# A row-mean kernel: the first load behind the entry barrier again, and the last row cut into columns of 704, 192 and 128

## The chip, the cores and the metric

The kernel runs on one core of a Trainium2 chip. Times are device microseconds of one execution. Three runs of the kernel before gave 163.88, 164.01 and 164.14 us; the median is 164.01. A profiled execution is read beside them.

## The reference

```python
def setup_inputs():
    batch, seq, dim = 32, 512, 1024
    return {"x": np.random.randn(batch, seq, dim).astype(np.float32)}

def reference(x):
    relu_x = np.maximum(x, 0)
    return np.mean(relu_x, axis=-1).astype(np.float32)
```

For each of 16384 rows of 1024 fp32 numbers the negative ones are set to zero and the mean is taken. The input is 67.1 MB, the output 64 KB.

## The kernel before

**Tiling.** The rows are laid out with 128 rows of `j` to each of 128 partitions: `J` is 128, and partition p holds rows 128 p to 128 p + 127. A tile `xt` takes 16 such rows per partition (`NB`, line 63), 128 x 16 x 1024 numbers, 8 MB. There are eight tiles and three buffers for them (line 72).

**Loads.** All loads are issued by SyncE. Seven tiles come in one DMA each (line 92). The eighth is cut finer and finer so that little work is left when the last byte lands: pieces of 8, 4, 2 and 1 rows (`row_pieces`, line 100), and the last row of each partition in three column pieces of 512, 256 and 256 (`col_pieces`, line 104). A load into a buffer waits until VectorE and ScalarE are done with the tile that was there.

**Compute.** Each row of a partition is one instruction that takes the maximum with zero in place and sums the row: odd rows on VectorE (`dve_row`, line 20), even rows on ScalarE (`act_row`, line 15). Each such instruction shows as two in the profile, the operation and a read of its accumulator. The sums go to a column of `sums`. GpSimd multiplies the sums by 1/1024 in two goes (`finish`, line 85): the first 112 columns once seven tiles are done, and 14 more in the last tile. The last two rows go their own way through the small tile `part`:

- The row before the last (`prev`) is halved between ScalarE and VectorE (lines 116 and 117); GpSimd adds the two parts and scales (line 118).
- The last row's first 512 columns are halved between ScalarE and VectorE (lines 121 and 122). GpSimd scales ScalarE's part (line 123). The next 256 are halved again (lines 126 and 127); VectorE's instruction takes its sum of the 256 before as a starting value (`init`), so it must wait for it. ScalarE adds its own part, scaled, to GpSimd's (line 128). The last 256 columns are VectorE's (line 131), started with the sum so far. VectorE's line 132 scales its sum and adds ScalarE's.

Line 135 stores the whole result, `res`, from SyncE.

**What sets the order.** Each engine takes its instructions in the order in which they were written, and semaphores set by the framework make an instruction wait for what it reads. At the start, line 155 (the program's creation) gives a few instructions ahead of the kernel's own: four GpSimd memsets of constants, and an entry barrier at which all five engines drain, report and wait for release. By hand, `issue_ahead_of_entry_barrier` (lines 26 to 42) takes SyncE's first load out of the kernel's body once all is compiled, and puts it in front of SyncE's drain at that barrier. The load waits for nothing, and its consumers wait for its semaphore.

Of the kernel before, what the change touches and what calls it, by code (L numbers as in the profile page):

```python
# [1 line left out]

# [4 lines left out]

F32 = mybir.dt.float32
ALU = mybir.AluOpType
ACT = mybir.ActivationFunctionType  # L10


def act_row(nc, src, acc):

    nc.scalar.activation(out=src, in_=src, func=ACT.Relu, accum_out=acc)  # L15


def dve_row(nc, src, acc, init=None):

    nc.vector.tensor_scalar(  # L20
        out=src, in0=src, scalar1=0.0, scalar2=init,
        op0=ALU.max, op1=ALU.add, accum_out=acc,
    )


def issue_ahead_of_entry_barrier(nc):


    entry, body = nc.cur_f.blocks[0].instructions, None
    for block in nc.cur_f.blocks[1:]:  # L30
        for k, ins in enumerate(block.instructions):
            if ins.opcode == "DMACopy":
                body, load = block.instructions, k
                break
        if body is not None:
            break
    first = body[load]
    assert first.engine == mybir.EngineType.SP and not first.sync_info.on_wait
    assert all(i.opcode == "DMACopy" or i.engine != first.engine for i in body[:load])
    del body[load]  # L40
    at = next(k for k, i in enumerate(entry) if i.engine == first.engine and i.opcode == "Drain")
    entry.insert(at, first)


@with_exitstack
def kernel(
    ctx: ExitStack,
    tc: tile.TileContext,
    x: bass.AP,
    out: bass.AP,  # L50
):
    nc = tc.nc
    P = nc.NUM_PARTITIONS
    xf = x.flatten_outer_dims()
    R, D = xf.shape
    assert R % P == 0
    J = R // P
    inv = 1.0 / D
    xr = xf.rearrange("(p j) d -> p j d", p=P, j=J)
    outr = out.flatten().rearrange("(p j) -> p j", p=P, j=J)  # L60
    xlast = xr[:, J - 1, :]

    NB = 16
    full = J // NB - 1

    row_pieces = [8, 4, 2, 1]
    assert sum(row_pieces) == NB - 1
    col_pieces = [512, 256, 256]
    assert sum(col_pieces) == D

    pools = ctx.enter_context(ExitStack())
    in_pool = pools.enter_context(tc.tile_pool(name="in", bufs=3))
    res_pool = pools.enter_context(tc.tile_pool(name="res", bufs=1))
    sums = res_pool.tile([P, J], F32)
    res = res_pool.tile([P, J], F32)
    part = res_pool.tile([P, 10], F32)

    def rows(xt, lo, n, j0):

        for k in range(lo, lo + n):  # L80
            j = j0 + k
            (dve_row if j % 2 else act_row)(nc, xt[:, k, :], sums[:, j:j + 1])

    def finish(lo, hi):
        nc.gpsimd.tensor_scalar(  # L85
            out=res[:, lo:hi], in0=sums[:, lo:hi], scalar1=inv, scalar2=0.0, op0=ALU.mult, op1=ALU.add,
        )

    for t in range(full):
        j0 = t * NB  # L90
        xt = in_pool.tile([P, NB, D], F32, name="xt")
        nc.sync.dma_start(out=xt, in_=xr[:, j0:j0 + NB, :])  # L92
        rows(xt, 0, NB, j0)

    j0 = full * NB
    xt = in_pool.tile([P, NB, D], F32, name="xt")
    prev, last = xt[:, NB - 2, :], xt[:, NB - 1, :]
    lo = 0
    for n in row_pieces:
        nc.sync.dma_start(out=xt[:, lo:lo + n, :], in_=xr[:, j0 + lo:j0 + lo + n, :])  # L100
        lo += n
    c = 0
    for w in col_pieces:
        nc.sync.dma_start(out=last[:, c:c + w], in_=xlast[:, c:c + w])
        c += w

    finish(0, j0)
    lo = 0
    for n in row_pieces[:-1]:
        rows(xt, lo, n, j0)  # L110
        lo += n
    finish(j0, j0 + lo)

    act_row(nc, prev[:, :512], part[:, 0:1])
    dve_row(nc, prev[:, 512:], part[:, 1:2])
    nc.gpsimd.tensor_scalar(  # L118
        out=res[:, J - 2:J - 1], in0=part[:, 0:1], scalar1=part[:, 1:2], scalar2=inv, op0=ALU.add, op1=ALU.mult,
    )  # L120
    act_row(nc, last[:, :256], part[:, 2:3])
    dve_row(nc, last[:, 256:512], part[:, 3:4])
    nc.gpsimd.tensor_scalar(  # L123
        out=part[:, 4:5], in0=part[:, 2:3], scalar1=inv, scalar2=0.0, op0=ALU.mult, op1=ALU.add,
    )
    act_row(nc, last[:, 512:640], part[:, 5:6])
    dve_row(nc, last[:, 640:768], part[:, 6:7], init=part[:, 3:4])
    nc.scalar.activation(  # L128
        out=part[:, 7:8], in_=part[:, 5:6], func=ACT.Identity, scale=inv, bias=part[:, 4:5],
    )  # L130
    dve_row(nc, last[:, 768:], part[:, 8:9], init=part[:, 6:7])
    nc.vector.scalar_tensor_tensor(  # L132
        out=res[:, J - 1:J], in0=part[:, 8:9], scalar=inv, in1=part[:, 7:8], op0=ALU.mult, op1=ALU.add,
    )
    nc.sync.dma_start(out=outr, in_=res)

    pools.close()
    tc.close()
    tc.compile()
    issue_ahead_of_entry_barrier(nc)  # L140


# [1 line left out]
_INS = ['x']  # L144
_OUTS = [((32, 512), 'float32')]


# [23 lines left out]
```

## Time and profile before

| | us |
|---|---|
| median of three runs | 164.01 |
| profiled execution | 163.88 |
| its span, first to last instruction | 162.1 |
| outside the span | 1.8 |
| VectorE busy | 74.7 |
| ScalarE busy | 69.6 |
| GpSimd busy | 1.2 |
| first tile landed | 22.34 |
| last column piece landed | 158.62 |
| last VectorE operation ends | 159.58 |

The times in the lower rows count from the span's start, which is SyncE's first load. Per row of 1024 columns VectorE takes 1.22 us and ScalarE 1.04 us. The DMA queue of the loads carries 67.18 MB, a mean of 415 GB/s over the span.

### The profile page before, as it was taken

The numbers are of one execution on the slowest core, as the hardware profiler recorded it, in microseconds if no ns is written. First come the engines' busy times: TensorE is split into PE (matmuls) and PEld (weight loads), VectorE is DVE, ScalarE is ACT, GpSimd is POOL, SyncE is SP. The second block draws the span as 40 slices with busy tenths as digits, with TensorE's granted clock in tenths as the row PEclk, the third lists the DMA queues.
The fourth block names the chain that finished last, engine by engine and source line by source line (L and its number), as shares of the span: only waits on it lengthen the run. The fifth ranks groups of instructions, "written<-read, shape, count | busy, mean of one in ns | idle before, by whom it ended". The sixth has DMA issues, their size and how long they took to land.

```text
span 162.1 us, 358 instructions
## 1 busy us (share of the span) xinstructions
DVE 74.7 (46%) x135; ACT 69.6 (43%) x134; POOL 1.2 (1%) x8
## 2 busy tenths in 40 slices
DVE  0000049700795009930199102990049800698993
ACT  3000049500793009910199002980049600696882
POOL 0000000000000000000000000000000000000001
DMA  8996996997997998998998999899898897998980
GB/s 275 501 485 291 518 501 291 501 501 323 469 518 340 437 518 356 420 518 356 420 520 374 404 501 404 388 501 404 388 518 388 388 518 332 437 445 384 420 311 17
DMA packets 2162, 67.19 MB, mean 415 GB/s; under 512 B 240, under 2 KB 624, under 8 KB 880
## 3 DMA queue, kind: packets, MB, share of 16 engines
q1 hardware_dynamic: 2160, 67.18, 96.6%
q14 instruction: 2, 0.02, 0.0%
HBM read 67.11 MB, written 0.07 MB: 414 GB/s over the span
## 4 chain that ended last, share of the span: by engine, by line
DMA 84%; DVE 13%; SPq 1%; issue 0%; DVEq 0%
DMA xt<-in_x_dram 84%; DVE xt L20 13%; SPq L100 1%; DVE res L132 0%; DVEq L20 0%; DVEq L132 0%; SPq L92 0%
## 5 line engine op out<-in xcount | busy, mean ns | idle before, releaser
L20 DVE TENSOR_SCALAR_CACHE_REDUCE xt<-xt 128x1024 f32<-128x1024 f32 (+1 forms) x65 | 73.7, 1195 | 84.7 <-DMA xt<-in_x_dram 84.3
L15 ACT ACTIVATE xt<-xt 128x1024 f32<-128x1024 f32 (+1 forms) x66 | 67.0, 1015 | 88.7 <-DMA xt<-in_x_dram 88.6
L15 ACT ACTIVATION_READ_ACCUMULATOR xt<-xt 128x1 f32 x66 | 12.3, 186 | 0.0
L20 DVE DVE_READ_ACCUMULATOR xt<-xt 128x1 f32 x65 | 5.4, 83 | 0.0
L85 POOL TENSOR_SCALAR res<-sums 128x112 f32<-128x112 f32 (+1 forms) x2 | 0.5, 252 | 156.7 <-DVE xt L20 156.7
L15 ACT ACT_TABLE_LOAD x1 | 1.3, 1283 | 0.8 <-PEq L155 0.8
L20 DVE TENSOR_SCALAR_CACHE_REDUCE xt<-xt,part 128x128 f32<-128x128 f32 (+1 forms) x2 | 0.8, 412 | 0.1
L128 ACT ACTIVATE part<-part 128x1 f32<-128x1 f32 x1 | 0.3, 294 | 0.1
L118 POOL TENSOR_SCALAR res<-part 128x1 f32<-128x1 f32 x1 | 0.3, 264 | 0.5 <-ACT xt L15 0.5
L132 DVE SCALAR_TENSOR_TENSOR res<-part 128x1 f32<-128x1 f32 x1 | 0.2, 159 | 0.1
L123 POOL TENSOR_SCALAR part<-part 128x1 f32<-128x1 f32 x1 | 0.2, 191 | 0.1
L20 DVE DVE_READ_ACCUMULATOR xt<-xt,part 128x1 f32 x2 | 0.2, 83 | 0.0
L155 POOL MEMSET const-bfloat16-1.0<- 128x1 bf16 x1 | 0.1, 101 | 0.0
L155 POOL MEMSET const-uint8-127<- 128x1 uint8 x1 | 0.1, 101 | 0.0
L155 POOL MEMSET const-float32-0.0<- 128x1 f32 x1 | 0.1, 98 | 0.2 <-issue 0.2
L155 POOL MEMSET const-float32-1.0<- 128x1 f32 x1 | 0.1, 98 | 0.0
## 6 DMA issues: line engine op xcount, KB each, us to landing
xt<-in_x_dram SPq DMA_DIRECT2D x1, 4096.0 KB, 39.0
xt<-in_x_dram SPq DMA_DIRECT2D x1, 2048.0 KB, 43.5
xt<-in_x_dram SPq DMA_DIRECT2D x1, 1024.0 KB, 45.5
xt<-in_x_dram SPq DMA_DIRECT2D x1, 512.0 KB, 46.4
xt<-in_x_dram SPq DMA_DIRECT2D x1, 256.0 KB, 46.5
xt<-in_x_dram SPq DMA_DIRECT2D x2, 128.0 KB, 42.7
xt<-in_x_dram SPq DMA_DIRECT2D x7, 49.1
out_dram<-res SPq DMA_DIRECT2D x1, 64.0 KB, 1.5
```

Of the source, the lines that this page charges most:

```text
L15: nc.scalar.activation(out=src, in_=src, func=ACT.Relu, accum_out=acc)
L20: nc.vector.tensor_scalar(out=src, in0=src, scalar1=0.0, scalar2=init, op0=ALU.max, op1=ALU.add, accum_out=acc,)
L85: nc.gpsimd.tensor_scalar(out=res[:, lo:hi], in0=sums[:, lo:hi], scalar1=inv, scalar2=0.0, op0=ALU.mult, op1=ALU.add,)
L100: nc.sync.dma_start(out=xt[:, lo:lo + n, :], in_=xr[:, j0 + lo:j0 + lo + n, :])
L118: nc.gpsimd.tensor_scalar(out=res[:, J - 2:J - 1], in0=part[:, 0:1], scalar1=part[:, 1:2], scalar2=inv, op0=ALU.add, op1=ALU.mult,)
L123: nc.gpsimd.tensor_scalar(out=part[:, 4:5], in0=part[:, 2:3], scalar1=inv, scalar2=0.0, op0=ALU.mult, op1=ALU.add,)
L128: nc.scalar.activation(out=part[:, 7:8], in_=part[:, 5:6], func=ACT.Identity, scale=inv, bias=part[:, 4:5],)
L132: nc.vector.scalar_tensor_tensor(out=res[:, J - 1:J], in0=part[:, 8:9], scalar=inv, in1=part[:, 7:8], op0=ALU.mult, op1=ALU.add,)
L155: nc = _bacc.Bacc("TRN2", target_bir_lowering=False, num_devices=1)
```

## The change

The changed kernel no longer moves the first load: `issue_ahead_of_entry_barrier` is gone, and so are the lines that closed the pools and compiled the program by hand ahead of it (the framework does both when the function returns). The last row comes in column pieces of 704, 192 and 128. ScalarE takes 416 columns of the first piece and VectorE 288; the other two pieces are VectorE's alone. No instruction starts with an earlier sum: each writes its own part. GpSimd adds the first three parts (new line 104) while VectorE works on the last piece, and VectorE adds the fourth part and scales (new line 108).

```diff
-def issue_ahead_of_entry_barrier(nc):
...
-    first = body[load]
...
-    del body[load]
-    at = next(k for k, i in enumerate(entry) if i.engine == first.engine and i.opcode == "Drain")
-    entry.insert(at, first)
...
-    col_pieces = [512, 256, 256]
+    col_pieces = [704, 192, 128]
...
-    act_row(nc, last[:, :256], part[:, 2:3])
-    dve_row(nc, last[:, 256:512], part[:, 3:4])
+    act_row(nc, last[:, :416], part[:, 2:3])
+    dve_row(nc, last[:, 416:704], part[:, 3:4])
+    dve_row(nc, last[:, 704:896], part[:, 4:5])
     nc.gpsimd.tensor_scalar(
-        out=part[:, 4:5], in0=part[:, 2:3], scalar1=inv, scalar2=0.0, op0=ALU.mult, op1=ALU.add,
+        out=part[:, 5:6], in0=part[:, 4:5], scalar1=part[:, 3:4], scalar2=part[:, 2:3], op0=ALU.add, op1=ALU.add,
     )
-    act_row(nc, last[:, 512:640], part[:, 5:6])
-    dve_row(nc, last[:, 640:768], part[:, 6:7], init=part[:, 3:4])
-    nc.scalar.activation(
-        out=part[:, 7:8], in_=part[:, 5:6], func=ACT.Identity, scale=inv, bias=part[:, 4:5],
-    )
-    dve_row(nc, last[:, 768:], part[:, 8:9], init=part[:, 6:7])
-    nc.vector.scalar_tensor_tensor(
-        out=res[:, J - 1:J], in0=part[:, 8:9], scalar=inv, in1=part[:, 7:8], op0=ALU.mult, op1=ALU.add,
+    dve_row(nc, last[:, 896:], part[:, 6:7])
+    nc.vector.tensor_scalar(
+        out=res[:, J - 1:J], in0=part[:, 6:7], scalar1=part[:, 5:6], scalar2=inv, op0=ALU.add, op1=ALU.mult,
     )
     nc.sync.dma_start(out=outr, in_=res)
-
-    pools.close()
-    tc.close()
-    tc.compile()
-    issue_ahead_of_entry_barrier(nc)
```

More of the change, by code (lines that the diff above doesn't have):

```diff
@@ L23, in dve_row @@
     )
-def issue_ahead_of_entry_barrier(nc):
[L29 to L36, printed above, removed]
-    first = body[load]
-    assert first.engine == mybir.EngineType.SP and not first.sync_info.on_wait
-    assert all(i.opcode == "DMACopy" or i.engine != first.engine for i in body[:load])
-    del body[load]
-    at = next(k for k, i in enumerate(entry) if i.engine == first.engine and i.opcode == "Drain")
-    entry.insert(at, first)
 @with_exitstack
@@ L67 @@
     assert sum(row_pieces) == NB - 1
-    col_pieces = [512, 256, 256]
+    col_pieces = [704, 192, 128]
     assert sum(col_pieces) == D
-    pools = ctx.enter_context(ExitStack())
-    in_pool = pools.enter_context(tc.tile_pool(name="in", bufs=3))
-    res_pool = pools.enter_context(tc.tile_pool(name="res", bufs=1))
+    in_pool = ctx.enter_context(tc.tile_pool(name="in", bufs=3))
+    res_pool = ctx.enter_context(tc.tile_pool(name="res", bufs=1))
     sums = res_pool.tile([P, J], F32)
```

## The prediction

> **What bounds the kernel now.** I read the slices of the page and the DMA share by stretches first, then the chain that ended last, then the two ends of the span instruction by instruction. The DMA share (columns: stretch, its length, busy VectorE, ScalarE and GpSimd, clock, DMA share, GB/s):
>
> ```profile
> 0.90:1.00 0.10, 0.00 (x0) 0.10 (x1) 0.00 (x0) 1.00 0.00 0
> 1.00:1.05 0.05, 0.00 (x0) 0.05 (x1) 0.00 (x0) 1.00 3.98 1311
> ...
> 2.00:138.00 136.00, 55.23 (x96) 50.60 (x97) 0.00 (x0) 1.00 0.99 428
> ```
>
> From 2 to 138 us the DMA engines are 0.99 busy and VectorE is busy for 55 us of 136. So the input stream runs without a hole: whatever delays its first byte delays every byte, and the compute engines have the slack to follow. The first byte moves at 1.01 us, one microsecond after the first issue at 0.00. The start, on SyncE and on ScalarE:
>
> ```profile
> 0.00 0.38 SPq L92 DMA_DIRECT2D xt<-in_x_dram  x1
> 0.78 0.33 SPq L92 DMA_DIRECT2D xt<-in_x_dram  x1
> 0.78 1.28 ACT L15 ACT_TABLE_LOAD   x1 [0.78 <-PEq L155]
> ```
>
> The first load goes out at 0.00, and the second only at 0.78, when the entry barrier (line 155) has let all engines go. The end of the span:
>
> ```profile
> 156.05 1.22 DVE L20 TENSOR_SCALAR_CACHE_REDUCE xt<-xt 128x1024 f32<-128x1024 f32 x1
> 157.19 0.08 DVE L20 DVE_READ_ACCUMULATOR xt<-xt 128x1 f32 x1
> 157.34 0.69 DVE L20 TENSOR_SCALAR_CACHE_REDUCE xt<-xt 128x512 f32<-128x512 f32 x1
> 157.95 0.08 DVE L20 DVE_READ_ACCUMULATOR xt<-xt 128x1 f32 x1
> 157.97 0.42 DVE L20 TENSOR_SCALAR_CACHE_REDUCE xt<-xt 128x256 f32<-128x256 f32 x1
> 158.32 0.08 DVE L20 DVE_READ_ACCUMULATOR xt<-xt 128x1 f32 x1
> 158.44 0.35 DVE L20 TENSOR_SCALAR_CACHE_REDUCE xt<-xt,part 128x128 f32<-128x128 f32 x1
> 158.71 0.08 DVE L20 DVE_READ_ACCUMULATOR xt<-xt,part 128x1 f32 x1
> 158.83 0.48 DVE L20 TENSOR_SCALAR_CACHE_REDUCE xt<-xt,part 128x256 f32<-128x256 f32 x1
> 159.23 0.08 DVE L20 DVE_READ_ACCUMULATOR xt<-xt,part 128x1 f32 x1
> 159.43 0.16 DVE L132 SCALAR_TENSOR_TENSOR res<-part 128x1 f32<-128x1 f32 x1
> ```
>
> The row before the last lands at 157.31 (in the chain: a DMA of 46.35 us from 110.96). The three column pieces are issued at 111.44, 111.93 and 119.59 and land 46.5, 46.4 and 39.0 us later: at 157.95, 158.31 and 158.62. The final operation ends at 159.58, so 0.96 us lie between the last byte and the last sum; then comes the store (issue at 159.65, landing 1.5 us later), and the span ends at 162.1.
>
> **Part 1: the first load goes back behind the barrier.** In the changed kernel's order of instructions SyncE passes the barrier's wait and then issues all seven big loads. The first issue takes the place that the second one has now, 0.78 us. It may be a little earlier: SyncE's drain, which the 0.38 us issue holds up, is the last arrival at the barrier (it ends at 0.56), and GpSimd's own drain after its four memsets ends at 0.49; without the early issue the barrier opens up to 0.07 us sooner. So the issue moves by 0.71 to 0.78 us; I take 0.71. From issue to first byte the trace has two rows: 1.01 us for this load, 0.84 us for the store (issue 159.65, first byte 160.49). If the load's longer time is a cold start that the wait at the barrier hides, 0.17 us come back. Lower bound of the shift 0.54, upper 0.78, taken **+0.71**, by the first row, which is the same load. Nothing covers it: the stream has no hole to absorb it. Loads 2 and 3 follow 0.38 and 0.8 us behind as now, and stand in the queue behind 19 us of transfer; load 4 goes out at 31.65, when a buffer is free, 29 us before load 3 has landed (61.0), and the later ones likewise. ScalarE's table load ends at 2.06, 20 us before the first data. No SyncE instruction is passed but the barrier's drain and wait.
>
> The Trainium skill ("DMA: Bandwidth & Descriptors", section Latency and other measured facts) gives about 600 ns to the first byte of a load issued from SyncE; the trace has 1010. If the page's figure held behind the barrier, the shift would be 0.71 + 0.60 - 1.01 = 0.30 us, an estimate from that page; I go by the row.
>
> **Part 2: column pieces 704, 192, 128.** The same 512 KB in the same three DMAs, so the last byte keeps its place, 158.62. The row's pieces took 1.31 us (157.31 to 158.62) for 1024 columns; in proportion 704 land after 0.90, at 158.21, and 192 at 158.46. Both engines, free at 157.97 and 158.02, now wait for the first piece until about 158.23; in before they begin at 157.97.
>
> **Part 3: the compute on the last row.** VectorE rows without a `part` input: 1024 columns 1.22 us, 512 0.69, 256 0.42, so 1.04 ns a column and 0.15 fixed; that makes 0.45 for 288, 0.35 for 192 and 0.285 for 128. In rows that wait for nothing the next one starts 0.07 us before the end of the one before (1.14 apart at 1.22 long). So 288 runs 158.23 to 158.68, 192 to 158.96, 128 to 159.17, its sum out at 159.18. What is removed is the wait of each piece for the sum of the one before: 0.04 us instead of -0.07 between pieces, and 0.06 us for reading `part` (0.48 against 0.42 for 256). ScalarE's 416 columns (rows 0.63 for 512, 0.42 for 256) take 0.55 and the accumulator read reaches 0.09 beyond: done at 158.87, ahead of VectorE's 192. ScalarE's two last operations (lines 126 and 128) go, off the path.
>
> The new wait: GpSimd's add of three parts (new line 104) stands behind VectorE's 192 sum at 158.97. Two GpSimd rows that wait for VectorE start 0.14 to 0.16 after it (157.43 after 157.28; 158.20 after ScalarE at 158.06): start 159.12. Its length is in no row: 0.19 with two constants (line 123), 0.26 with one pointer (line 118), so between 0.19 and 0.34 with two pointers (0.07 more for the second); I take 0.30: 159.42. VectorE's last operation waits for it; semaphore to start is 0.06 (SyncE's store behind line 132) to 0.11 (ScalarE's line 128 behind line 123): 159.48 to 159.53. VectorE's own 128 sum would allow 159.18 + 0.11 = 159.29, so **GpSimd ends last, not VectorE**. The last operation is 0.16 by line 132, up to 0.22 if its pointer costs what it cost the 256 piece. End 159.64 to 159.75, against 159.58. Bounds for the tail: below, all low values, 159.05 + 0.19 + 0.06 + 0.16 = 159.46, or -0.12; above, +0.20. Taken **+0.06**. Behind it only SyncE's store is queued, which moves with it.
>
> The Trainium skill ("Perfetto Trace Analysis", section GPSIMD Engine Instruction) says to treat GpSimd spans as unreliable and go by start to start. ScalarE's line 128 starts 0.30 us after GpSimd's line 123, at most 0.11 us after its shown end, so the trace has no hidden end there; by starts alone the add would cost 0.30 + 0.07 and the tail some +0.06 to +0.1.
>
> **Sum.** 0.71 + 0.06 = +0.77 us on the profiled execution's 163.88: 164.65 (its span would grow less, since the span begins with the first instruction, which is now no longer the load). The median of the three runs stands 0.13 above that execution, 164.01, so the forecast is 164.01 + 0.77, about **164.8**.
>
> **Rivals.**
> 1. *An instruction fetch sets the end (not slower).* Tiles land every 19.32 to 19.35 us, but 80.36 to 100.22 is 19.86: 0.51 more, the stretch in which the page's two packets of queue q14 fall. The 0.51 us stays to the end. If in the changed program the fetch falls where it doesn't hit the DMA engine that is last, 0.51 comes back: 0.71 + 0.06 - 0.51 = +0.26, 164.27, no measurable change. It decides from 0.44 us given back. Against it: VectorE and ScalarE run the same 126 row operations in the same order until the last row, so they fetch at the same place. Chance 0.07. The Trainium skill ("Runtime: NRT & Kernel Launch", section Instruction fetch mechanics) calls the fetch mostly hidden; by it this rival is worth nothing, and the row of 0.51 us disagrees.
> 2. *Half the start is hidden.* The first packets take longer than later ones: the first tile lands at 22.34, 21.3 us after its first byte, against 19.35 for later tiles. If part of this ramp is a clock of its own and not part of the load, up to 0.4 us of it could run beside the barrier: 164.4. For: 2 us of ramp is much. Against: nothing moves bytes before the issue. Chance 0.07.
> 3. *The tail is dearer*: GpSimd's two-pointer add takes 0.5 us or more, or its start lags: +0.3 and more, 165.05 to 165.3. Chance 0.07.
> 4. *Faster*: the early issue brings nothing now (the queue not ready before 1.0 us, whatever the issue) and independent sums save 0.12: at most 163.9 to 163.6. Against it: the store's row shows at least 0.84 us from issue to byte, so a load issued at 0.71 cannot move before 1.55. Chance 0.03.
>
> **How the numbers follow.** The forecast has 0.76. Its own bounds are 164.01 + 0.54 - 0.12 = 164.43 and 164.01 + 0.78 + 0.20 = 164.99, with 0.13 us of spread between runs on each side at worst; the range 164.35 to 165.1 holds it and parts of rivals 2 and 3, about 0.83 in all. A measurement tells 0.2% from no change, 0.33 us, so slower means above 164.34. Rival 1 and a small part of 2 fall within (0.09), rival 4 gives 0.03 faster, the rest 0.88 slower.
>
> **What would show it.** Right: the SyncE row of the first load behind the barrier, with the bytes 1.0 us behind it; the final VectorE operation released by GpSimd's line 104, about 1.0 us after the last column piece. Wrong: bytes less than 0.8 us after the issue (part 1), tile landings without the 19.86 step (rival 1), a last operation that starts straight behind VectorE's 128 piece (part 3).

## The result and the profile after

The changed kernel takes 164.69 us (median of four runs, 164.59 to 165.03) against 163.97 for the one before in the same measurement; the ratio is 1.0046, interval 1.0028 to 1.0064. That is slower by 0.72 us; the forecast was 0.79 (164.8 against 164.01). Its profiled execution took 164.59 us with a span of 162.8; the one before took 163.88 with 162.1. Both spans begin at the same moment of the entry (VectorE's drain lies 0.13 us behind it in both), so times within the spans may be compared.

The start, DMA share by stretches as before, then the first issue on SyncE and the table load on ScalarE:

```profile
1.60:1.70 0.10, 0.00 (x0) 0.10 (x1) 0.00 (x0) 1.00 0.00 0
1.70:1.75 0.05, 0.00 (x0) 0.05 (x1) 0.00 (x0) 1.00 8.13 2621
...
2.00:138.00 136.00, 55.23 (x96) 50.55 (x97) 0.00 (x0) 1.00 0.99 428
```

```profile
0.73 0.38 SPq L72 DMA_DIRECT2D xt<-in_x_dram  x1
0.73 1.28 ACT L15 ACT_TABLE_LOAD   x1 [0.73 <-PEq L126]
```

The issue has moved from 0.00 to 0.73 us, the first byte from 1.01 to 1.74. The barrier opens 0.05 us sooner than before (the table load starts at 0.73 instead of 0.78), where up to 0.07 was forecast, since SyncE no longer comes to it late. The stream is as full as it was: 0.99, 428 GB/s.

The last row, in order of time (start, length, engine and line):

```profile
157.92 0.69 DVE L20 TENSOR_SCALAR_CACHE_REDUCE xt<-xt 128x512 f32<-128x512 f32 x1
158.53 0.08 DVE L20 DVE_READ_ACCUMULATOR xt<-xt 128x1 f32 x1
...
158.82 0.45 DVE L20 TENSOR_SCALAR_CACHE_REDUCE xt<-xt 128x288 f32<-128x288 f32 x1 [0.21 <-DMA xt<-in_x_dram]
...
159.20 0.35 DVE L20 TENSOR_SCALAR_CACHE_REDUCE xt<-xt 128x192 f32<-128x192 f32 x1
159.28 0.19 ACT L15 ACTIVATION_READ_ACCUMULATOR xt<-xt 128x1 f32 x1
159.47 0.08 DVE L20 DVE_READ_ACCUMULATOR xt<-xt 128x1 f32 x1
159.47 0.28 DVE L20 TENSOR_SCALAR_CACHE_REDUCE xt<-xt 128x128 f32<-128x128 f32 x1
159.68 0.08 DVE L20 DVE_READ_ACCUMULATOR xt<-xt 128x1 f32 x1
159.73 0.36 POOL L104 TENSOR_SCALAR part<-part 128x1 f32<-128x1 f32 x1 [0.68 <-DVE xt L20]
160.13 0.21 DVE L108 TENSOR_SCALAR res<-part 128x1 f32<-128x1 f32 x1 [0.37 <-POOL part L104]
```

VectorE now waits 0.21 us for the first column piece. Its pieces follow each other without a gap, and its last sum is out at 159.76, but it then stands idle for 0.37 us until GpSimd's add of three parts is done at 160.10. The column pieces land at 158.80, 159.01 and 159.20, so from the last landing to the end of the last operation (160.35) it is 1.15 us, against 0.97 before.

Put together, after against before in these two executions: first byte +0.73; first tile landed +0.83 (23.17 against 22.34), so 0.10 more from the first byte to the first landing; the stretch between the fourth and the fifth tile 19.61 instead of 19.86, so -0.25; last column piece +0.58; the work behind it +0.18; the store and the exit -0.05. The sum is +0.71, the whole difference of 164.59 and 163.88.

### The profile page after: what moved, and what is told of

Read it like the earlier page. It is cut to its first block, busy times and chain, and to the rows that moved or that the text cites. A ratio compares the mean times of both kernels' runs of the same rounds, so it can differ in the third digit from the quotient of the medians.

```text
span 162.8 us, 353 instructions
## 1 busy us (share of the span) xinstructions
DVE 74.5 (46%) x135; ACT 69.2 (43%) x131; POOL 1.3 (1%) x8
## 4 chain that ended last, share of the span: by engine, by line
DMA 84%; DVE 12%; SPq 1%; issue 0%; POOLq 0%; DVEq 0%
DMA xt<-in_x_dram 84%; DVE xt L20 12%; SPq L80 1%; POOLq L137 0%; SPq L72 0%; DVE res L108 0%; DVEq L20 0%; POOLq L104 0%
## 5 line engine op out<-in xcount | busy, mean ns | idle before, releaser
L20 DVE TENSOR_SCALAR_CACHE_REDUCE xt<-xt 128x1024 f32<-128x1024 f32 (+2 forms) x67 | 74.2, 1169 | 85.5 <-DMA xt<-in_x_dram 85.1
```

Source lines behind the costliest of these rows:

```text
L20: nc.vector.tensor_scalar(out=src, in0=src, scalar1=0.0, scalar2=init, op0=ALU.max, op1=ALU.add, accum_out=acc,)
```

## The experiments

Eleven runs. "Tail" is the time from the last landing to the end of the last operation in the run's profile.

| run | load | tail in the profile, us | time, us | ratio to before, interval |
|---|---|---|---|---|
| before | ahead of the barrier | 0.97 | 163.81 to 163.97 | |
| after | behind | 1.15 | 164.69 | 1.0046, 1.0028 to 1.0064 |
| e1_load_behind | behind | 0.98 | 164.33 | 1.0038, 1.0026 to 1.0050 |
| e2_tail_alone | ahead | 1.14 | 163.98 | 1.0012, 1.0004 to 1.0021 |
| e3_two_parts | ahead | 1.06 | 163.88 | 1.0012, 1.0002 to 1.0022 |
| e7_one_piece | ahead | 0.83 | 163.74 | 0.9992, 0.9983 to 1.0001 |
| e5_scalar_ends | ahead | 0.78 | 163.73 | 0.9990, 0.9980 to 0.9999 |
| e12_scalar_again | ahead | 0.78 | 163.60 | 0.9986, 0.9977 to 0.9995 |
| e6_few_rows (no compute on two tiles) | ahead | 0.98 | 164.01 | 1.0010, 1.0001 to 1.0020 |
| e9_fewest_rows (no compute on four tiles) | ahead | 0.99 | 163.98 | 1.0003, 0.9994 to 1.0012 |
| e8_load_later | behind a memset | 0.98 | 166.91 | 1.0179, 1.0165 to 1.0194 |
| e10_first_row | 1 row ahead | 0.81 | 163.57 | 0.9985, 0.9969 to 1.0000 |
| e11_first_four | 4 rows ahead | 0.81 | 163.27 | 0.9965, 0.9954 to 0.9977 |

**Start alone and tail alone.** The first run undoes only the early issue in the kernel before:

```diff
     tc.compile()
-    issue_ahead_of_entry_barrier(nc)
```

> The kernel before, with only the moving of the first load taken away. Theory (start and tail add up): the first issue at about 0.73 us, the first byte 1.0 us behind it, every landing later by 0.7 to 0.85, the work behind the last column piece unchanged at 0.96 us; time +0.55 to +0.85 us over before. Rival (the start is partly hidden and the new tail is most of the loss): +0.1 to +0.4 us.

The second keeps the early issue and takes the new tail. Against the changed kernel it puts the early issue back:

```diff
+def issue_ahead_of_entry_barrier(nc):
...
+    pools.close()
+    tc.close()
+    tc.compile()
+    issue_ahead_of_entry_barrier(nc)
```

> The changed kernel, with the first load ahead of the barrier as before: the new tail alone. Theory: 1.15 us from the last landing to the end of the last operation as in the changed kernel, 0.18 more than before, so +0.1 to +0.25 us if the last landing stays. Rival (the tail costs nothing, all is the start): within 0.05 us of before. Second rival (the tail is most of the loss): +0.4 us or more.

Behind the barrier alone costs a ratio of 1.0038, 0.62 us; the new tail alone 1.0012, 0.20 us. Their sum, 0.82, agrees with the 0.75 of both together (1.0046) within the intervals. The start is about three quarters of that sum, and the rivals of both runs fall: the start is neither mostly hidden nor the smaller part, and the tail is not free. The issue stands at 0.74 and the first byte at 1.75 in the first run; in the second the tail is that of the changed kernel instruction by instruction. One thing in the first run missed: every landing was to come 0.7 to 0.85 us later, but in the profiled executions the first tile lands 0.56 later (22.90) and the last piece 0.42 (159.04). From first byte to first landing it took 21.15 us there, in the kernel before 21.33; that differs from run to run, as the next run shows too.

**A larger dose of the start.** The load waits, behind the barrier, for a VectorE memset of cells that it then fills (so do the next two loads):

```diff
+        if t < 3:
+            nc.vector.memset(xt[:, 0:2, :], 0.0)
         nc.sync.dma_start(out=xt, in_=xr[:, j0:j0 + NB, :])
...
-    issue_ahead_of_entry_barrier(nc)
```

> The kernel before without the early issue, and the first three loads wait besides for a VectorE memset of 2048 columns each in the tiles they fill (nothing left out). Theory (the input stream has no hole, so the start goes into the time one for one): the first byte 1.0 us behind the issue, and the last landing later than with the load merely behind the barrier by as much as the issue is later (1.1 to 2.2 us by the memset's unknown length), within 0.35 us for the ramp. Rival (a ramp with a clock of its own): the first tile's landing moves by less than half of what the issue moves.

The first rows on VectorE and SyncE:

```profile
1.24 1.76 DVE L93 MEMSET xt<- 128x2048 f32 x1 [1.24 <-PEq L156]
3.03 4.61 SPq L94 DMA_DIRECT2D xt<-in_x_dram  x3
```

The issue is at 3.03, 2.29 us later than merely behind the barrier; the first byte is at 4.05. By the ratios the kernel takes 2.93 us more than before (2.70 to 3.18), and 2.31 more than with the load merely behind the barrier. So the start goes into the time one for one, as near as these intervals tell. From first byte to first landing it takes 21.6 us here, 21.2 (first run) and 21.4 (changed kernel) behind the barrier, and 21.1 to 21.4 in the kernels with the uncut load ahead: it is no shorter when the load waits, so no part of it runs beside the barrier. In the profiled executions the last landing is later by 2.72 us than in the first run, 0.43 more than the issue, where at most 0.35 was expected; 0.40 of it is the longer time to the first landing.

**Who ends the tail.** The three-part add is taken apart: GpSimd adds the two parts of the first piece only, and VectorE reads the 192 sum as one more cell of the last piece. For that the 192 columns are now the row's last ones, and are loaded ahead of the 128. Against the kernel with the new tail alone:

```diff
...
-    for w in col_pieces:
...
+    for lo, hi in ((0, 704), (832, 1024), (704, 832)):
...
-    dve_row(nc, last[:, 704:896], part[:, 4:5])
     nc.gpsimd.tensor_scalar(
-        out=part[:, 5:6], in0=part[:, 4:5], scalar1=part[:, 3:4], scalar2=part[:, 2:3], op0=ALU.add, op1=ALU.add,
+        out=part[:, 5:6], in0=part[:, 2:3], scalar1=part[:, 3:4], scalar2=inv, op0=ALU.add, op1=ALU.mult,
     )
-    dve_row(nc, last[:, 896:], part[:, 6:7])
+    dve_row(nc, last[:, 832:], last[:, 703:704])
+    dve_row(nc, last[:, 703:832], part[:, 6:7])
...
```

> The new tail with the load ahead of the barrier, but GpSimd adds only the two parts of the first piece (one pointer, no need of the 192 columns), and VectorE carries the 192 sum into the last piece by a column in front of it. Theory (GpSimd's add of three parts, waiting for the 192 sum, ends last): the last operation is released by VectorE's own last piece, 0.75 to 0.95 us from the last landing to its end, 0.2 to 0.4 less than with three parts. Rival (VectorE's own chain sets the end, the wait for GpSimd is only named last): no less than 1.1 us.

```profile
158.36 0.35 DVE L20 TENSOR_SCALAR_CACHE_REDUCE xt<-xt 128x192 f32<-128x192 f32 x1
158.60 0.26 POOL L119 TENSOR_SCALAR part<-part 128x1 f32<-128x1 f32 x1 [0.51 <-ACT xt L15]
158.64 0.08 DVE L20 DVE_READ_ACCUMULATOR xt<-xt 128x1 f32 x1
158.75 0.29 DVE L20 TENSOR_SCALAR_CACHE_REDUCE xt<-xt 128x129 f32<-128x129 f32 x1
158.97 0.08 DVE L20 DVE_READ_ACCUMULATOR xt<-xt 128x1 f32 x1
159.16 0.16 DVE L124 SCALAR_TENSOR_TENSOR res<-part 128x1 f32<-128x1 f32 x1
```

GpSimd is done at 158.86 and no longer in the way, yet the tail is 1.06, between the 0.75 to 0.95 of my theory and the 1.1 of its rival. VectorE's own waits take the place: the 192 columns start at 158.36 instead of right behind the 288 at 158.24, since they write a cell that the 288 wrote, and the 129 start 0.04 us behind the end of the 192 instead of 0.07 ahead of it. Counted from the start of the 288 the last piece begins 0.89 us later, in the changed tail 0.65. That eats what GpSimd's add cost there: VectorE's own sum was out at 159.76, and 0.11 us later (the step to line 132 in the kernel before) its last operation could have started, 0.26 us sooner than it did; this is an estimate from those rows. So GpSimd's add does end the changed tail, but this edit gains only 0.08 us in the tail, and none in the time.

**A tail without those waits.** If waits from sum to sum are the cost and columns are not, fewer instructions are better. First, 192 and 128 as one piece; GpSimd adds the two parts of the first piece, as in the run before:

```diff
-    col_pieces = [704, 192, 128]
+    col_pieces = [704, 320]
...
+    dve_row(nc, last[:, 704:], part[:, 6:7])
...
```

> The load ahead of the barrier; the last row in pieces of 704 and 320; the 320 are one VectorE instruction that waits for no earlier sum, GpSimd adds the two parts of the first piece and VectorE adds the rest. Theory (the tail is paid in waits from sum to sum, some 0.1 us each, and not in columns): 0.80 to 0.90 us from the last landing to the end of the last operation, against 1.14 in the changed tail, 0.97 in the one before and 1.06 with two parts and a third piece; released by GpSimd or VectorE within 0.1 us of one another; time 0.05 to 0.2 us under before. Rival (columns after the last landing set the tail): 320 columns in one pass are 0.2 us more than 128, so 1.1 us or more.

```profile
158.47 0.49 DVE L20 TENSOR_SCALAR_CACHE_REDUCE xt<-xt 128x320 f32<-128x320 f32 x1
158.82 0.27 POOL L123 TENSOR_SCALAR part<-part 128x1 f32<-128x1 f32 x1 [0.49 <-ACT xt L15]
158.88 0.08 DVE L20 DVE_READ_ACCUMULATOR xt<-xt 128x1 f32 x1
159.12 0.16 DVE L127 SCALAR_TENSOR_TENSOR res<-part 128x1 f32<-128x1 f32 x1 [0.15 <-POOL part L123]
```

Then ScalarE as the last engine: the two sums of the first piece go into the two cells ahead of the second one, and one scaled ScalarE instruction sums cells and columns straight into the result.

```diff
+    head = 448
...
+    act_row(nc, flat[:, mid:c0 + D], flat[:, c0 - 2:c0 - 1])
+    dve_row(nc, flat[:, c0 + head:mid], flat[:, c0 - 1:c0])
+    end = flat[:, c0 - 2:c0 + head]
+    nc.scalar.activation(out=end, in_=end, func=ACT.Relu, scale=inv, accum_out=res[:, J - 1:J])
```

> The load ahead of the barrier; the last row in two pieces of 576 and 448, in that order; ScalarE and VectorE sum 288 columns each of the first and put their sums into the two cells in front of the second piece, and one ScalarE instruction sums those cells and the 448 columns, scaled, into the result. No GpSimd or VectorE work behind the last landing. Theory (waits from engine to engine are the tail): 0.70 to 0.80 us from the last landing to the end, the shortest of all tails; time 0.1 to 0.3 us under before. Rival (the ScalarE pass of 450 columns eats what the waits give back): 0.97 us or more, time as before.

```profile
158.44 0.58 ACT L124 ACTIVATE xt<-xt 128x450 f32<-128x450 f32 x1
158.92 0.19 ACT L124 ACTIVATION_READ_ACCUMULATOR xt<-xt 128x1 f32 x1
159.17 0.35 SPq L125 DMA_DIRECT2D out_dram<-res  x1
```

> The kernel whose last operation is ScalarE's, unchanged, once more: the base of the two runs with a cut first load, and a second measurement against before. Theory: 0.78 us from the last landing to the end as in its first run, time 0.05 to 0.3 us under before. Rival (its first result was chance): time as before.

The tails are 0.83 and 0.78 (0.78 again in the repeat), with 320 and 450 columns behind the last landing, against 1.14 with 128. In the tail the theory holds: three small pieces pay for their waits, not for their columns. In time, one piece comes out at 0.9992 (not told from before) and ScalarE's end at 0.9990 and 0.9986, some 0.2 us under before.

**The instruction packets.** Two kernels leave out the computation of tiles 1 and 2, or 1 to 4, so those columns of the result stay zero; all is loaded.

```diff
...
-        rows(xt, 0, NB, j0)
+        if t not in (1, 2):
+            rows(xt, 0, NB, j0)
```

> The kernel before, but tiles 1 and 2 are loaded and not computed (their 32 columns of the result are left at zero), so VectorE and ScalarE have 16 row operations fewer each. Theory (the instruction packets that lengthen one stretch between landings come with the engines' place in their instructions): no packet of queue q14 between 80 and 90 us, and either none at all or later or earlier by many us; if none, all landings 19.35 us apart and the end 0.25 to 0.5 us sooner, 163.4 to 163.8. Rival (the packets come with time or with another engine, not with the two engines' row operations): the same packets near 84 to 88 us and the same longer stretch, time as before.

> The kernel before, but tiles 1 to 4 are loaded and not computed (their 64 columns of the result are left at zero), so VectorE and ScalarE have 32 row operations fewer each. With 16 fewer the two instruction packets came 38.7 us later, two tiles, at the same place in the two engines' rows, in the 37th or so. Theory: now fewer than 36 rows are left per engine, so no such packet comes at all, all landings are 19.3 to 19.4 us apart but for chance, and the time is 0.2 to 0.5 us under before. Rival (the packets are not what lengthens the stretch): packets or none, one stretch is 0.25 to 0.5 us longer again and the time is as before.

The queue of the instruction packets (packets, MB, share of 16 engines), first from 119.3 to 139.0 us of the kernel without tiles 1 and 2, then from 148.2 to 153.4 us of the one without 1 to 4:

```profile
q14 instruction: 2, 0.02, 0.2%
...
q14 instruction: 2, 0.02, 0.8%
```

The instructions up to the first packet, counted from 20 us, which is ahead of the first row operation (stretch, its length, busy time and number of instructions on VectorE, ScalarE and GpSimd, clock, DMA share, GB/s): the kernel before, then the two kernels:

```profile
20.00:84.28 64.28, 31.39 (x55) 29.08 (x55) 0.00 (x0) 1.00 0.99 430
20.00:123.11 103.11, 31.34 (x55) 29.02 (x55) 0.00 (x0) 1.00 1.00 432
20.00:152.10 132.10, 31.47 (x55) 29.16 (x55) 0.29 (x1) 1.00 0.99 429
```

With 16 row operations fewer per engine the two packets move from 84 and 87 us to 123 and 126, two tiles later; with 32 fewer, to 152. So they did not go away, which I had expected of the last kernel. The count shows why: when the first packet comes, 55 instructions have begun on each of the two engines in all three kernels, 28 row operations and 27 reads of the accumulator. I had put the place in the 37th row or so, and the last kernel still has 35 row operations on VectorE and 34 on ScalarE. In all thirteen profiles each packet comes in the 28th or 30th row operation of VectorE and the 28th, 30th or 31st of ScalarE. So their place goes with the work of these two engines and not with the time; which of the two fetches, and why some packets come two rows later than others, stays open.

Wherever they come, that stretch is longer: 119.27 to 139.06 is 19.79 us instead of 19.35, and 148.11 to 153.41 is 5.30 instead of 4.89, while 80 to 100 us is 19.3 in both. In all the runs with full work that stretch is 0.24 to 0.51 us longer. But some stretches without packets are longer too (60.85 to 80.61 us of the kernel without tiles 1 and 2 is 19.76), and as the packets stayed, no run shows the time of a kernel without them.

**A shorter ramp.** The idea was that the DMA engine that starts last sets the landings. The trace does not name a packet's engine, but in the kernel before the first 16 packets of the load start between 1.01 and 2.16 us, ahead of the end of any of them, so they should be one on each of the 16 engines. Two runs on top of ScalarE's tail cut the first load (shown with four rows; the other has 1 in place of 4):

```diff
-        nc.sync.dma_start(out=xt, in_=xr[:, j0:j0 + NB, :])
+        cut = 4 if t == 0 else NB
+        nc.sync.dma_start(out=xt[:, :cut, :], in_=xr[:, j0:j0 + cut, :])
+        if cut < NB:
+            nc.sync.dma_start(out=xt[:, cut:, :], in_=xr[:, j0 + cut:j0 + NB, :])
```

> The kernel whose last operation is ScalarE's (the tail with the shortest end so far), with the first tile's load cut in two: one row of each partition ahead of the barrier, the other 15 behind it. Theory (the engine that starts last sets the end of the stream, and it starts 0.8 to 1.25 us behind the first because the descriptors of a big load are made engine after engine): with 4 KB for each partition the last engine starts less than 0.5 us behind the first, all 8 MB of the first tile land 0.3 to 0.7 us sooner than 22.1 to 22.3, and the time is 0.3 to 0.7 us under the same kernel without the cut. Rival (the spread of starts comes back with the second load, or the small load runs out before the second is issued): the first tile lands at 22.1 or later, time the same or up to 0.5 us more.

> The same, with four rows of each partition ahead of the barrier and 12 behind it, so that the first load lasts about 5 us and cannot run out. Theory: the spread of starts goes by descriptors of the first load, so it lies between that of one row and that of 16; a gain of 0.1 to 0.5 us. Rival (the spread does not depend on the size of the load): last engine 0.8 to 1.25 us behind the first, time as without the cut.

With one row the 16th packet starts 0.35 us behind the first (the first to end does so just before that, so the last engine may start a little later), with four rows 0.73, and uncut, in the two runs of the same kernel, 1.25 and 1.55. The whole first tile has landed at 22.10, 21.85, and 22.18 and 22.42. Four rows give 163.27 us, 0.9965 of before (0.9954 to 0.9977), against 0.9986 without the cut: 0.35% under the kernel before, and under the changed one. One row is not told from no cut (0.9985; its runs scatter from 163.28 to 164.63, and one took 165.89), so its theory, 0.3 to 0.7 us of gain, missed, and its rival (the first tile at 22.1 us or later, no gain) came out. Its spread is the smallest, but in the profiled executions its tile lands 0.25 us later than with four, about as much as the two executions of the uncut kernel lie apart. The small load does not run out: in its trace the packets under way add up to those of 16 engines, 15.7 at the least in slices of 0.2 us, from 1.5 to 6 us. In both cut kernels the first 16 packets of the second load again start 0.65 to 0.7 us apart. So why four rows do better than one is open. That the spread of the starts is what the cut gains by is not shown, nor is the theory's reason for the spread, descriptors made engine after engine.

## Why the prediction was right, point by point

- **Part 1, the start.** Taken +0.71 by the issue row; the issue moved by 0.73 and the first byte by 0.73, the load's own 1.01 us from issue to byte stayed 1.01. The lower bound, 0.54, rested on the store's 0.84 us; no first load here was that fast (1.0 us in all thirteen profiles). Alone it measured +0.62 us (0.43 to 0.82). The Trainium skill ("DMA: Bandwidth & Descriptors", section Latency and other measured facts) has about 600 ns to the first byte; the first load of every run here shows 1.0 us, on both sides of the barrier.
- **The span.** I wrote that the span would grow less than the time, as it would no longer begin with the load. It grew by the same 0.71: SyncE's drain now stands where the load stood.
- **Part 2, the pieces.** 704 columns were put 0.41 us ahead of the last landing, and it was 0.40.
- **Part 3, the tail.** The order was right: GpSimd's add ends after VectorE's own sum, and VectorE's last operation waits for it. The lengths of VectorE's 288, 192 and 128 columns were right within 0.01 us. The mis-sized term is the price of pointers: the add takes 0.365 us, not 0.30 (no pointer 0.19, one 0.26, two 0.365, so the second costs 0.10, not 0.07), and the last operation 0.21, not 0.16. GpSimd starts 0.18 us after the 192 sum, not 0.14 to 0.16, and from its end to VectorE's start it is 0.03, not 0.06 to 0.11. Besides, +0.06 was the low end of the prediction's own 159.64 to 159.75, which is +0.06 to +0.17. So the tail is +0.18 in the profile and 0.20 us in time (0.07 to 0.34), where +0.06 was taken; in the profile it lies within the bound of +0.20, the interval of the time reaches beyond it.
- **Rival 1, the fetch.** It did not come out, but a piece of it did: the stretch is 19.61 us instead of 19.86 in the profiled execution, 0.25 of the 0.51, in a program whose rows are the same up to there. Both packets come at 87.3 us, in the 30th row operation of VectorE, where before they came at 84.3 and 86.7, in the 28th and the 30th; so the argument that the engines fetch at the same place held but for two rows. This hides a part of the loss in that execution; over all runs the stretch scatters from 19.59 to 19.86. The Trainium skill ("Runtime: NRT & Kernel Launch", section Instruction fetch mechanics) calls such a fetch mostly hidden; here the stretch it falls into is 0.24 to 0.51 us longer each time.
- **Rivals 2 to 4.** No part of the ramp runs beside the barrier (by the ratios the dose of 2.29 us came out as 2.31). In the profile the tail was not dearer than its bound. The early issue did bring the bytes forward.

The forecast's sum, 0.77, was near the measured 0.72 to 0.75 with a start too large by some 0.1 (0.71 against 0.62, within its interval) and a tail too small by 0.14. That the two offset one another was luck.

## What to carry to other kernels

Where the stream of loads is full from the first byte to the last, the first issue counts one for one; look at it before the compute. How the first load is cut can count too (four rows first: 0.2% here). At the end, count waits from sum to sum (some 0.1 us each here) and pointer operands ahead of columns: one longer instruction that takes earlier sums in as cells of its input can end sooner than three short ones. A change of two parts is best measured as two: here both made it slower, and one alone was about three quarters.

## What was not expected of the hardware

- The first 16 packets of the first load start one after the other, and the spread goes by the load's size: 0.35 us for 4 KB a partition, 0.73 for 16 KB, 0.8 to 1.6 for 64 KB. How much of it lasts to the end of the stream is not shown: in the profiled executions with four rows the first tile lands 0.33 and 0.57 us before that of the two uncut ones, the last piece 0.25 and 0.31.
- The stretch into which two instruction packets of 8 KB each fall is 0.24 to 0.51 us longer, in all thirteen profiles. They come with VectorE's 28th and 30th row operation, whatever the time.
- Four executions have a further stretch that is longer by 0.2 to 0.4 us without such packets (the third tile of the kernel with the new tail alone took 19.70 us); what causes it was not found.
